# A direct dependency on ScalarE in place of a one-element copy ahead of two late loads in a softmax kernel

## The chip, the cores and the metric

One core of one Trainium2 chip. The metric is the device time of one execution in microseconds, as the median of several executions. All executions told here are counted as fast ones; the one core's granted clock is 1.0 in every record. Execution times of one kernel spread by a few tenths of a microsecond (by 1.6 us in one experiment, and this is said there). The span of a profile runs from the first to the last instruction and is some 1.8 us shorter than the execution time of the same run. Every experiment is compared with the kernel before, run in the same rounds. Where its edit is against the changed kernel, that rests on the two being equal in time.

## The reference, cut to what matters

```python
# x: float32 [16, 1024, 512]
x_scaled = x / 0.5
x_max = np.max(x_scaled, axis=-1, keepdims=True)
exp_x = np.exp(x_scaled - x_max)
return exp_x / np.sum(exp_x, axis=-1, keepdims=True)
```

16384 rows of 512 numbers: 33.55 MB are read and 33.55 MB are written.

## The kernel before

The rows are cut into eight chunks, each 128 partitions by 16 rows (4.19 MB). VectorE takes the row maxima, ScalarE makes the exponentials and their sums, and VectorE and ScalarE together multiply by the reciprocal sums. There are six buffers, so the seventh and eighth chunk reuse the first and the second. SyncE issues the loads and ScalarE issues the stores. The eighth chunk comes in two parts: SyncE loads 15 of its 16 rows as soon as the second buffer is free, and GpSimd loads the last row (one per partition, 0.26 MB) later.

```python
LOADS = [[(0, 4), (4, G)]] + [WHOLE] * 6 + [[(0, G - 1)]]
BLOCKS = [[(0, 4), (4, 8), (8, G)]] + [WHOLE] * 6 + [[(0, 8), (8, G)]]
STORES = [WHOLE] * 8
...
    def load_last_row(signal):
        seen = stats.tile([P, 1], fp32, name="seen", bufs=1)
        copied = nc.gpsimd.tensor_copy(out=seen, in_=signal)
        finished.append(copied.ins.name)
        c = C - 1
        ...
        for p0, p1 in ((P - 2, P), (0, P - 2)):
            part = nc.gpsimd.dma_start(
                out=to[p0:p1], in_=of_[p0:p1], max_dma_last_dim=2 * D
            )
            finished.append(part.ins.name)
...
        for g in rows:                      # in exponentials(i, rows)
            row = chunks[c][:, lo + g, :]
            nc.scalar.activation(
                out=row, in_=row, func=EXP,
                bias=biases[i][:, g : g + 1], scale=2.0,
                accum_out=sums[i][:, g : g + 1],
            )
            if c == BUFS - 1 and g == 10:
                load_last_row(sums[i][:, g : g + 1])
```

The copy's result is never used. Its job is to stand in GpSimd's queue ahead of the two loads and to hold them there until ScalarE has written the sum of row 10 of the sixth chunk. The list `finished` is what a final no-operation on SyncE waits for.

## Time and profile before

| | before |
|---|---|
| execution time, median of 3 runs | 161.86 us (161.72 to 161.98) |
| span of the profile | 160.5 us (of an execution of 162.29 us) |
| VectorE, ScalarE, GpSimd busy | 134.6, 102.2, 1.9 us |
| moved by transfers | 67.13 MB, mean 418 GB/s |

In the profile DVE is VectorE, ACT is ScalarE, POOL is GpSimd and SP is SyncE; a name with q is the engine's instruction queue. A line of the timeline has the start, the length, the engine, the line of the kernel and the operation, and in brackets the idle time before it and what ended that. The main views are shown in the prediction below. One line is added here: the last wait of SyncE's queue, with its total, its number and its longest in us.

```profile
SPq L205 <- DMA out_dram<-xt: 9.5, 1, 9.5
```

It begins just after the seventh chunk's store has landed and ends when the last one has. A store of 4.19 MB in 9.5 us is 441 GB/s, no slower than the stretches of full engines in the prediction's table (417 to 439 GB/s).

### The profile page before, as it was taken

How to read it: one execution, taken by the hardware profiler on the slowest of the kernel's cores; microseconds unless marked ns; L12 is line 12 of the kernel's file. 1: busy time of each engine (PE TensorE's matmuls, PEld its weight loads, DVE VectorE, ACT ScalarE, POOL GpSimd, SP SyncE). 2: the span in 40 equal slices, each digit the busy share in tenths (PEclk: the TensorE clock that was granted, in tenths of full speed). 3: DMA queues.
4: the chain of work that ended last, by engine and by line, in shares of the span. 5: the costliest groups of instructions: out<-in, count | busy, mean ns of one | idle time of the engine just before them, and what ended most of it. 6: DMA issues, size and time to landing. Idle time of an engine off the chain costs nothing.

```text
span 160.5 us, 411 instructions
## 1 busy us (share of the span) xinstructions
DVE 134.6 (84%) x45; ACT 102.2 (64%) x273; POOL 1.9 (1%) x7
## 2 busy tenths in 40 slices
DVE  0607999999999999999999999999999999957000
ACT  3071549069989963998199909991899891790000
POOL 0000000000000000000000000030000000000000
DMA  5999999999989999999999999989999999999994
GB/s 184 470 408 498 400 392 457 457 392 402 506 269 425 490 392 400 506 400 392 490 425 392 474 434 392 490 383 483 422 450 400 400 465 441 392 457 449 400 441 204
DMA packets 2578, 67.13 MB, mean 418 GB/s; under 512 B 328, under 2 KB 328, under 8 KB 400
## 3 DMA queue, kind: packets, MB, share of 16 engines
q1 hardware_dynamic: 1296, 33.29, 49.3%
q10 hardware_dynamic: 1152, 33.55, 48.4%
q0 software_dynamic: 128, 0.26, 0.4%
q14 instruction: 2, 0.02, 0.0%
HBM read 33.55 MB, written 33.55 MB: 418 GB/s over the span
## 4 chain that ended last, share of the span: by engine, by line
DVE 75%; DMA 7%; issue 5%; ACT 3%; SPq 0%
DVE negmax L77 42%; DVE xt L127 31%; DMA xt<-in_x_dram 7%; ACT xt L108 3%; DVE bias L81 1%; DVE recip L125 1%; SPq L68 0%
## 5 line engine op out<-in xcount | busy, mean ns | idle before, releaser
L108 ACT ACTIVATE xt<-xt,bias 128x512 f32<-128x512 f32 x128 | 90.4, 708 | 41.5 <-DVE bias L81 40.6
L77 DVE TENSOR_REDUCE negmax<-xt 128x16 f32<-128x8192 f32 (+2 forms) x11 | 69.9, 6352 | 9.4 <-DMA xt<-in_x_dram 9.4
L127 DVE TENSOR_TENSOR xt<-xt,recip 128x7168 f32<-128x7168 f32 (+2 forms) x11 | 62.0, 5637 | 0.4
L108 ACT ACTIVATION_READ_ACCUMULATOR xt<-xt,bias 128x1 f32 x128 | 23.9, 187 | 0.0
L138 ACT ACTIVATE xt<-xt,recip 128x512 f32<-128x512 f32 x15 | 9.9, 706 | 0.0
L125 DVE RECIPROCAL recip<-sums 128x16 f32<-128x16 f32 (+2 forms) x11 | 2.4, 218 | 1.8 <-ACT xt L108 1.8
L81 DVE TENSOR_SCALAR bias<-negmax 128x16 f32<-128x16 f32 (+2 forms) x11 | 1.9, 173 | 0.4
L52 ACT ACT_TABLE_LOAD x1 | 1.3, 1283 | 0.7 <-PEq L194 0.7
L97 POOL DMA_DIRECT2D xt<-in_x_dram x2 | 1.5, 741 | 0.5 <-issue 0.5
L90 POOL COPY seen<-sums 128x1 f32<-128x1 f32 x1 | 0.2, 184 | 103.6 <-ACT xt L108 103.6
L51 DVE MEMSET warm<- 128x1 f32 x1 | 0.1, 59 | 0.8 <-PEq L194 0.8
L52 ACT ACTIVATE warm<-warm 128x1 f32<-128x1 f32 x1 | 0.2, 202 | 0.0
L194 POOL MEMSET const-float32-0.0<- 128x1 f32 x1 | 0.1, 93 | 0.2 <-issue 0.2
L194 POOL MEMSET const-bfloat16-1.0<- 128x1 bf16 x1 | 0.1, 95 | 0.0
L194 POOL MEMSET const-uint8-127<- 128x1 uint8 x1 | 0.1, 95 | 0.0
L194 POOL MEMSET const-float32-1.0<- 128x1 f32 x1 | 0.1, 93 | 0.0
## 6 DMA issues: line engine op xcount, KB each, us to landing
out_dram<-xt ACTq DMA_DIRECT2D x8, 4096.0 KB, 23.1
xt<-in_x_dram SPq DMA_DIRECT2D x6, 4096.0 KB, 34.8
xt<-in_x_dram SPq DMA_DIRECT2D x1, 3840.0 KB, 27.8
xt<-in_x_dram SPq DMA_DIRECT2D x1, 3072.0 KB, 11.6
xt<-in_x_dram SPq DMA_DIRECT2D x1, 1024.0 KB, 4.8
xt<-in_x_dram POOLq DMA_DIRECT2D x1, 252.0 KB, 15.4
xt<-in_x_dram POOLq DMA_DIRECT2D x1, 4.0 KB, 9.1
```

The source lines that it names most:

```text
L51: nc.vector.memset(warm, 0.0)
L52: nc.scalar.activation(out=warm, in_=warm, func=EXP)
L77: nc.vector.tensor_reduce(negmax[:, 0:b], chunks[c][:, lo:hi, :], axis=AX, op=MAX, negate=True)
L81: nc.vector.tensor_scalar_mul(biases[i][:, 0:b], negmax[:, 0:b], 2.0)
L90: copied = nc.gpsimd.tensor_copy(out=seen, in_=signal)
L97: part = nc.gpsimd.dma_start(out=to[p0:p1], in_=of_[p0:p1], max_dma_last_dim=2 * D)
L108: nc.scalar.activation(out=row, in_=row, func=EXP, bias=biases[i][:, g : g + 1], scale=2.0, accum_out=sums[i][:, g : g + 1],)
L125: nc.vector.reciprocal(recips[i][:, 0:b], sums[i][:, 0:b])
L127: last = nc.vector.tensor_mul(rows, rows, recips[i][:, 0:k].unsqueeze(2).broadcast_to((P, k, D)))
L138: last = nc.scalar.activation(out=row, in_=row, func=COPY, scale=recips[i][:, g : g + 1])
L194: nc = _bacc.Bacc("TRN2", target_bir_lowering=False, num_devices=1)
```

## The change

The copy goes, and with it GpSimd's only arithmetic in the loop. Both loads are given a dependency on the exponential by hand. The intent is a shorter way from ScalarE to the loads and an engine less that reads memory.

```diff
     def load_last_row(signal):
-        seen = stats.tile([P, 1], fp32, name="seen", bufs=1)
-        copied = nc.gpsimd.tensor_copy(out=seen, in_=signal)
-        finished.append(copied.ins.name)
         c = C - 1
 ...
             part = nc.gpsimd.dma_start(
                 out=to[p0:p1], in_=of_[p0:p1], max_dma_last_dim=2 * D
             )
+            tc.add_manual_dep(part.ins, signal, info, reason="in step")
             finished.append(part.ins.name)
 ...
-            nc.scalar.activation(
+            exponential = nc.scalar.activation(
 ...
             if c == BUFS - 1 and g == 10:
-                load_last_row(sums[i][:, g : g + 1])
+                load_last_row(exponential.ins.name)
```

(The definition of `info` moves from the end of the kernel to its start.)

More of the change, by code (lines that the diff above doesn't have):

```diff
@@ L59 @@
     finished = []
+    info = mybir.DependencyInfo(
+        mybir.DependencyClass.Sync, mybir.DependencyReason.DATA
+    )
     def load(c):
@@ L174 @@
     seen = nc.sync.nop()
-    info = mybir.DependencyInfo(
-        mybir.DependencyClass.Sync, mybir.DependencyReason.DATA
-    )
     for name in finished:
```

## The prediction

> **What bounds the kernel now.** I read the page first, then the transfer shares by stretch, then the chain of the end, then what waits on GpSimd. The page says that two things are full at once:
>
> ```profile
> span 160.5 us, 411 instructions
> DVE 134.6 (84%) x45; ACT 102.2 (64%) x273; POOL 1.9 (1%) x7
> DMA  5999999999989999999999999989999999999994
> HBM read 33.55 MB, written 33.55 MB: 418 GB/s over the span
> DVE 75%; DMA 7%; issue 5%; ACT 3%; SPq 0%
> ```
>
> The reader is to see that the transfers are at nine tenths or more in nearly every slice, and that GpSimd (POOL) is busy for 1.9 us of 160.5. The chain of the end gives 75% to VectorE (DVE), but a chain goes back from an instruction to its releaser; it doesn't show a queue of transfers that is never empty. For that I cut the span by hand, at the times where the late loads and the last store begin and land (columns: stretch, length, busy time of DVE, ACT and POOL, clock, DMA share, GB/s):
>
> ```profile
> 88.00:104.09 16.09, 16.02 (x5) 12.08 (x35) 0.00 (x1) 1.00 1.01 434
> 104.82:106.30 1.48, 1.48 (x1) 1.48 (x5) 1.48 (x2) 1.00 0.97 417
> 106.30:120.90 14.60, 14.53 (x5) 10.59 (x29) 0.00 (x0) 1.00 1.02 436
> 120.90:132.83 11.93, 11.86 (x5) 11.44 (x30) 0.00 (x0) 1.00 1.02 439
> ...
> 140.00:147.48 7.48, 5.57 (x3) 4.46 (x12) 0.00 (x0) 1.00 0.98 425
> 147.48:150.10 2.62, 0.00 (x0) 0.00 (x0) 0.00 (x0) 1.00 0.93 400
> 150.10:159.70 9.60, 0.00 (x0) 0.00 (x0) 0.00 (x0) 1.00 0.88 379
> ```
>
> From 88 us on the 16 engines move 417 to 439 GB/s without a gap. The last store (4.19 MB) is issued at 147.48 and lands 12.2 us later, at about 159.7. From 147.48 to 159.70 the table gives 2.62 us x 400 + 9.60 us x 379 = 4.69 MB, some 0.5 MB more than that store: an estimate of what the store before it still had to move when it was issued, a good microsecond at 434 GB/s. So VectorE, which ends at 147.4, and the transfers reach the end together; neither alone would give much back.
>
> The part that is changed, in order of time:
>
> ```profile
> 103.84 0.18 ACT L108 ACTIVATION_READ_ACCUMULATOR xt<-xt,bias 128x1 f32 x1
> 103.86 8.68 DVE L77 TENSOR_REDUCE negmax<-xt 128x16 f32<-128x8192 f32 x1
> 103.93 0.71 ACT L108 ACTIVATE xt<-xt,bias 128x512 f32<-128x512 f32 x1
> 104.09 0.18 POOL L90 COPY seen<-sums 128x1 f32<-128x1 f32 x1 [103.64 <-ACT xt L108]
> ...
> 104.82 1.48 POOL L97 DMA_DIRECT2D xt<-in_x_dram  x2 [0.55 <-issue]
> ```
>
> The exponential of row 10 of the sixth chunk delivers its sum at 103.84 + 0.18 = 104.02. The copy starts 0.07 us later and ends at 104.27; then GpSimd sits idle for 0.55 us for nothing that the profile shows, and makes the descriptors of its two loads until 106.30. The row these loads bring is needed only by the last row maximum, which starts at 132.83:
>
> ```profile
> xt<-in_x_dram POOLq DMA_DIRECT2D x1, 252.0 KB, 15.4
> xt<-in_x_dram POOLq DMA_DIRECT2D x1, 4.0 KB, 9.1
> L77 DVEq EVENT_SEMAPHORE  x1: 21/21/21, 125.3 to 125.3; - x1
> L205 POOLq DRAIN  x3: 40/103/15775, 105.3 to 160.2; - x3
> 132.83 4.41 DVE L77 TENSOR_REDUCE negmax<-xt 128x8 f32<-128x4096 f32 x1
> ```
>
> The larger load, issued at 105.5, lands 15.4 us later, at 120.9; the drain on GpSimd's queue agrees (105.3 + 15.8 = 121.1). VectorE's only separate semaphore wait at that line, at 125.3, lasts 21 ns: what it asks for is there already. So the load is 4.4 us ahead of the check and 132.83 - 120.9 = 11.9 us ahead of use. That is the slack that everything below must be held against.
>
> **What the Trainium skill says.** First, "DMA: Bandwidth & Descriptors", section "Issuing engines are not separate DMA queues": transfers issued from ScalarE, SyncE or GpSimd all run on the same 16 engines and interleave, and issuing from several only saves issue time. The trace agrees: the rate is 417 to 439 GB/s with GpSimd's queue in use and without. Second, the same page's "Specifications" gives a ceiling of 435 GB/s for the fabric; the 434 to 439 here (a few per cent of rounding at the cut edges) are at it. Third, "SBUF — State Buffer", section "Who interferes with whom": a VectorE instruction with two SBUF inputs contends with a GpSimd instruction that reads SBUF, while a reduction doesn't contend. The copy reads SBUF, and VectorE's two-input product ended at 96.32 + 7.62 = 103.94, just before the copy; during the descriptors VectorE runs a reduction. So no clash shows in this trace, and none is there to be removed. Fourth, "Perfetto Trace Analysis", section "DMA Instruction — SWDGE (GPSIMD)": the profile's end of such an instruction is the last descriptor written, not the data's landing. The trace agrees: 0.70 and 0.78 us for the instructions, against 9.1 and 15.4 us to landing.
>
> **The change part by part.** (1) Removed: one copy of 128x1, 0.18 us on GpSimd, which is idle for 103.6 us before. On the path of the end: 0. VectorE and ScalarE don't wait for it; the waits list has no waiter on GpSimd's copy. (2) Moved: the wait for ScalarE goes from the copy to the loads themselves. It is the same event at the same 104.02, since the copy too was released by this exponential. The loads also had to wait for the second chunk's store, which was over by about 88 us (the SyncE queue issued the other fifteen rows into the same buffer at 88.0); that wait stays and costs nothing. (3) The issue of the first load: at least the copy's 0.18 us goes. Of the 0.55 us of idle after it, part is the queue's own semaphore instruction (43 ns) and presumably the decoding of the load, which stays. So the first descriptors start between 104.1 (all goes: 0.73 us earlier) and 104.65 (only the copy goes); I choose 104.5, about 0.3 us earlier. If nothing else moves, the larger load lands at 120.6 rather than 120.9, and its slack grows from 11.9 to 12.2 us. Value at the end: 0. (4) Transfers: the same 0.26 MB in the same 128 packets, out of 67.13 MB. With the engines full before and after, 0.3 us earlier for 0.4% of the bytes only trades places with bytes of the loads and stores beside it. (5) The final wait on SyncE has one item less to wait for, the copy. It waits for the seventh chunk's store until 150.1 anyway, and the program's end waits on the last store until 159.7. Value: 0. (6) The start-up fills of constants on GpSimd (four of 0.09 us) stay, so the start doesn't move. Sum on the path: 0 + 0 + 0 + 0 + 0 = 0 us, out of 161.86.
>
> **The rivals.** (a) The order is lost: if the new dependency held only one load, or none, the loads would go at about 88 us, when the buffer comes free, 16 us earlier. For it: the dependency is now set by hand, not implied by data. Against it: the final wait is set in the same way and does hold in this trace. Its effect: the queue is as full at 88 us (434 GB/s) as at 104, so bytes trade places again; the other fifteen rows land a little later, still before 125.3. Within 0.3 us of now, either sign. (b) The copy was a cushion: without it the descriptors could run into VectorE's product, and stall or slow it. The product ends at 103.94 and the release is at 104.02, so the margin is under 0.1 us, but ScalarE's schedule decides it and is not changed. If they met, the skill's section speaks of reads only, and descriptors are written; at worst 0.7 us on VectorE, of which about one microsecond of queued store hides most. To 162.3 at most. (c) A change of order among transfers opens a gap. Between 116 and 125 us only the fifth chunk's store and these loads are in flight, and the next store comes at 125.43; the bytes are the same, so a gap would be there before too. Worth under 0.2 us. (d) The path of the end does run through GpSimd in a way that the profile hides; then up to 0.73 us would be saved: 161.1. The 11.9 us of slack speak against it.
>
> **Range and chances.** The sum is zero, so the prediction is the time before, 161.86, rounded to 161.8. The three runs spread from 161.72 to 161.98; other executions and the rivals add about as much again on either side: 161.5 to 162.2 should hold it 8 times in 10. A change of 2% is 3.2 us, over four times all that the change can move on GpSimd. No rival reaches it. Faster by over 2%: 0.01; within 2%: 0.98; slower by over 2%: 0.01.
>
> **What would show it.** GpSimd is to have 6 busy instructions instead of 7, about 1.7 us, and no copy; its first load starts between 104.1 and 104.65 and is now said to wait for ScalarE. Its larger load lands at 120.2 to 120.8. VectorE's last reduction starts at 132.8, the last store is issued at 147.5 and the DMA row is unchanged. Wrong would be: loads at 88 us (rival a), a product of 128x7168 longer than 7.63 us next to the descriptors (rival b), a DMA share under 0.95 between 116 and 126 us (rival c), or an end moved by as much as the loads (rival d).

## The result, and the profile after

| | before | after |
|---|---|---|
| median of 6 runs | 161.88 us (161.72 to 161.99) | 162.07 us (161.80 to 162.44) |
| ratio after to before, 95% interval | | 1.0013 (0.9997 to 1.0029) |
| span of the profile | 160.5 us (execution of 162.29 us) | 160.5 us (execution of 162.30 us) |
| GpSimd busy | 1.9 us, 7 instructions | 1.7 us, 6 instructions |

A ratio here and below is the mean time of one kernel's fast runs over that of the other's of the same rounds, so it isn't quite the ratio of the medians quoted. The interval contains 1: no change is shown.

The page of the changed kernel, in the lines that answer to those of before (busy time by engine, the transfers' row of 40 slices, and the two late loads with KB and us from issue to landing):

```profile
DVE 134.6 (84%) x45; ACT 102.2 (64%) x273; POOL 1.7 (1%) x6
DMA  5999999999999999999999999999999999999993
xt<-in_x_dram POOLq DMA_DIRECT2D x1, 252.0 KB, 15.9
xt<-in_x_dram POOLq DMA_DIRECT2D x1, 4.0 KB, 9.1
```

The timeline around the changed place:

```profile
103.88 0.19 ACT L109 ACTIVATION_READ_ACCUMULATOR xt<-xt,bias 128x1 f32 x1
103.90 8.68 DVE L80 TENSOR_REDUCE negmax<-xt 128x16 f32<-128x8192 f32 x1
...
104.36 1.47 POOL L97 DMA_DIRECT2D xt<-in_x_dram  x2 [103.92 <-ACT xt L109]
...
132.86 4.41 DVE L80 TENSOR_REDUCE negmax<-xt 128x8 f32<-128x4096 f32 x1
```

And three lines of what the instruction queues did: GpSimd's separate semaphore instructions of the loads (length in ns as least, median, longest; first and last start), its drain at the end in the same form, and SyncE's last wait:

```profile
L97 POOLq EVENT_SEMAPHORE  x2: 17/30/42, 87.4 to 87.5; - x2
```

```profile
L203 POOLq DRAIN  x3: 40/107/16265, 104.9 to 160.3; - x3
```

```profile
SPq L203 <- DMA out_dram<-xt: 9.5, 1, 9.5
```

The copy is gone and the loads now name ScalarE as what released them. ScalarE's sum is there at 103.88 + 0.19 = 104.07, and descriptors begin at 104.36: 0.29 us, against 0.80 us before (104.02 to 104.82). The wait for the buffer's store has been moved ahead, to 87.4, so the load itself waits for ScalarE alone. But the larger load, issued at 105.1, takes 15.9 us in place of 15.4 and lands at 121.0, not earlier than the 120.9 of before; the drain agrees (104.9 + 16.3 = 121.2). Nothing that lies behind it moved: the last reduction starts at 132.86 (before: 132.83) and SyncE's last wait is 9.5 us in both. So in these traces the half microsecond was won on GpSimd, spent again in the engines' queues, and would have been worth nothing at the end in any case.

### The profile page after: what moved, and what is told of

Read it like the earlier page. It is cut to its first block, busy times and chain, and to the rows that moved or that the text cites. A ratio compares the mean times of both kernels' runs of the same rounds, so it can differ in the third digit from the quotient of the medians.

```text
span 160.5 us, 411 instructions
## 1 busy us (share of the span) xinstructions
DVE 134.6 (84%) x45; ACT 102.2 (64%) x273; POOL 1.7 (1%) x6
## 4 chain that ended last, share of the span: by engine, by line
DVE 75%; DMA 7%; issue 5%; ACT 3%; SPq 0%
DVE negmax L80 42%; DVE xt L128 31%; DMA xt<-in_x_dram 7%; ACT xt L109 3%; DVE bias L84 1%; DVE recip L126 1%; SPq L71 0%
## 6 DMA issues: line engine op xcount, KB each, us to landing
xt<-in_x_dram POOLq DMA_DIRECT2D x1, 252.0 KB, 15.9
```

## The experiments

The theory: the late loads are off the path that sets the end, with some 12 us of slack, and the end is set by transfers that never pause, with VectorE close behind. The rivals: a path through GpSimd that the profile doesn't show, a cost of the time at which these loads enter, and a clash of GpSimd with VectorE.

### The changed kernel again

No edit.

> The changed kernel once more, for a narrower interval. Theory (the late loads have 11.9 us of slack, and the engines that move data are full either way): ratio 1.000, between 0.998 and 1.002, and the larger late load lands at about 121 us whether its issue is at 104.4 or 104.8. Rival (the first six runs, 162.07 against 161.88, show a real cost of the change): ratio 1.0013 again with the interval above 1.0000.

Measured: 161.85 us (161.70 to 161.90, 5 runs) against 161.94 us (161.84 to 162.13, 9 runs), ratio 0.9991 (0.9979 to 1.0004). The first table's +0.1% is not repeated; its sign turns. Both intervals contain 1. The difference of the first table is noise as far as these runs can tell. The larger late load's time from issue to landing is repeated: 15.8 us, with the landing at 120.8.

### No step at all

```diff
-            tc.add_manual_dep(part.ins, signal, info, reason="in step")
```

> The dependency on the exponential is taken away; the late loads wait only until the store of their buffer has landed. Theory: they are issued at about 88 us, 16 us earlier, land at 98 to 108 us, and the time stays within 0.3 us of 161.9, because the same bytes go through full engines. Rival (the step is there because early loads push back the load beside them or the stores): slower by 1 us or more, with the other fifteen rows landing after 125.3 us or VectorE waiting for a transfer.

Measured: 162.22 us (162.08 to 162.32) against the same 161.94, ratio 1.0014 (1.0002 to 1.0027). The timeline, and the page's line of the larger load:

```profile
88.37 1.47 POOL L97 DMA_DIRECT2D xt<-in_x_dram  x2 [87.92 <-DMA out_dram<-xt]
```

```profile
xt<-in_x_dram POOLq DMA_DIRECT2D x1, 252.0 KB, 21.0
```

The loads go 16 us earlier. The larger one, issued at 89.1, needs 21.0 us and lands at 110.1, later than the 98 to 108 expected, and the time is 0.28 us longer by the medians, within the 0.3 us expected; the interval is just clear of 1. The rival's full microsecond isn't there, and VectorE waits for no transfer but the two at the start that every run has (9.5 us in all). This is what the kernel would do if the new dependency had been lost: next to nothing.

### Thirty-two copies in place of one

```diff
-        copied = nc.gpsimd.tensor_copy(out=seen, in_=signal)
+        for _ in range(32):
+            copied = nc.gpsimd.tensor_copy(out=seen, in_=signal)
```

> The kernel before with 32 copies of the sum in place of one. At 0.18 us each, 31 more are 5.6 us, so the loads are issued at about 110.5 us. Theory: the larger load lands at 122 to 129 us, before its use at 132.8, and the time is unchanged, ratio 0.998 to 1.002. Rival (the end runs through GpSimd): plus up to 5.6 us, 167.5 us.

Measured: 161.81 us (161.68 to 161.91), ratio 0.9991 (0.9978 to 1.0005).

```profile
104.11 7.76 POOL L91 COPY seen<-sums 128x1 f32<-128x1 f32 x32 [103.66 <-ACT xt L109]
112.42 1.48 POOL L98 DMA_DIRECT2D xt<-in_x_dram  x2 [0.56 <-issue]
...
132.84 4.41 DVE L77 TENSOR_REDUCE negmax<-xt 128x8 f32<-128x4096 f32 x1
```

```profile
xt<-in_x_dram POOLq DMA_DIRECT2D x1, 252.0 KB, 13.1
```

The thirty-two copies take 7.76 us, some 0.24 us each and not 0.18, and push the loads to 112.42, past the 110.5 expected. The larger one is issued at 113.1, needs 13.1 us and lands at 126.2, still before the last reduction, which starts at 132.84 as ever. GpSimd's part was made 7.6 us longer (112.42 against 104.82) and the end didn't move: the interval contains 1. The rival of a hidden path through GpSimd falls here: taking 0.5 us from GpSimd cannot help where adding 7.6 us doesn't hurt. The idle 0.56 us between the last copy and the loads is there again as it was with one copy.

### No late loads

```diff
-    LOADS = [[(0, 4), (4, G)]] + [WHOLE] * 6 + [[(0, G - 1)]]
+    LOADS = [[(0, 4), (4, G)]] + [WHOLE] * 7
...
-            if c == BUFS - 1 and g == 10:
+            if False:
```

> No late loads on GpSimd at all: the last chunk comes as one load of 16 rows on the SyncE queue. Theory: 161.9 us within 0.4, since the bytes are the same and the whole load lands at 116 to 119 us, before the check at 125.3. Rival (the late row buys time by leaving the queue to others): slower by over 0.5 us.

Measured: 162.27 us (162.16 to 162.35), ratio 1.0018 (1.0006 to 1.0031). As expected within 0.4 us, but clear of 1. So the whole device of a separate last row on GpSimd is worth at most some 0.3 us here, 0.2%. That is also about the spread of one kernel: the profiled execution of the kernel before, which isn't among the nine, took 162.29 us. With the run without a step it suggests that the row is a little dearer when it goes in at 88 us with the others. What makes these 0.3 us is not settled: VectorE's timing doesn't explain it, since in this run the last store was issued at 147.36, 0.12 us earlier than before.

### The step at row 5: with the copy, and direct

The kernel before and the changed kernel, each with this edit:

```diff
-            if c == BUFS - 1 and g == 10:
+            if c == BUFS - 1 and g == 5:
```

> The kernel before with row 5 in place of row 10 as the trigger, its exponential ending near 100.5, in the middle of VectorE's product of two inputs (96.3 to 103.9). If the copy is shut out by the product: it starts or ends only at 104 and the loads are issued at 104.8 as before. If not: copy at 100.6, loads at 101.3. The time is unchanged in either case, 161.9 within 0.4.

> The changed kernel with row 5 as the trigger, so that descriptors are made while VectorE's product of two inputs runs. Theory[...]: loads at 100.8, 0.7 us each, product still 7.62 us, time unchanged within 0.4 us. Rival b of the prediction: descriptors take until 104, or the product is longer than 7.7 us.

Measured: with the copy 161.81 us (161.75 to 162.06), ratio 0.9992 (0.9977 to 1.0007); direct 161.84 us (161.84 to 162.00), ratio 0.9991 (0.9974 to 1.0008). The times tell nothing; the traces do. With the copy:

```profile
96.22 7.62 DVE L127 TENSOR_TENSOR xt<-xt,recip 128x7168 f32<-128x7168 f32 x1
...
100.47 3.42 POOL L90 COPY seen<-sums 128x1 f32<-128x1 f32 x1 [100.02 <-ACT xt L108]
...
103.83 1.48 POOL L97 DMA_DIRECT2D xt<-in_x_dram  x2
```

Direct:

```profile
96.33 7.62 DVE L128 TENSOR_TENSOR xt<-xt,recip 128x7168 f32<-128x7168 f32 x1
...
100.82 1.47 POOL L97 DMA_DIRECT2D xt<-in_x_dram  x2 [100.37 <-ACT xt L109]
```

The reader is to compare the copy's 3.42 us with its 0.18 us in the kernel before. It begins inside VectorE's product of two inputs and ends at 100.47 + 3.42 = 103.89, the product at 96.22 + 7.62 = 103.84: the copy of 128 numbers was held until the product was over, and the loads behind it with it. This is the exclusive use that the Trainium skill states in "SBUF — State Buffer", section "Who interferes with whom", for a GpSimd instruction that reads. The product was not slowed: 7.62 us in both. The descriptors of the loads, in contrast, take the same 1.47 us in the middle of the product as outside of it. So the clash of the prediction's rival b is real, but it belongs to the copy that was removed and not to the loads. In the kernel before, the copy came 0.15 us after the product's end (104.09 against 103.94), so there was nothing to save at row 10. One more thing shows: behind the held copy the loads follow without the 0.55 us of idle time that they have behind a short one (103.89, then 103.83 as recorded), so that idle time isn't a fixed price of following a copy. What it is stays open.

### The step later than the slack

In the changed kernel, for the two runs:

```diff
-            if c == BUFS - 1 and g == 10:
+            if c == BUFS and g == 10:                      # first run
+            if c == C - 1 and lo == 0 and g == 2:          # second run
```

> The dependency is on row 10 of the seventh chunk, whose exponential ends near 120.7, so the late loads are issued 16.5 us later than in the changed kernel, at about 121 to 122. Theory (slack is to 132.8): the loads by then share the engines with stores only and land near 131 to 134, so the end moves by 0 to 1.5 us. If the landing still took 15.9 us: it is at 137.7 and the end moves by about 4 us.

> The dependency is on row 2 of the last chunk, whose exponential ends near 128.2. Theory: issued at about 129, landing at 138 to 144, after the use at 132.8; VectorE waits 5 to 11 us for the transfer and the time grows by 4 to 10 us, 166 to 172 us. If the late loads had no bearing on the end at any time: 0.

Measured: first 162.94 us (162.19 to 163.80, 4 runs) against 161.96, ratio 1.0060 (1.0013 to 1.0108); second 171.07 us (170.68 to 171.40), ratio 1.0560 (1.0535 to 1.0584). The first, in four views (timeline; the reduction's semaphore instruction; transfers by stretch with columns as in the prediction; the page's line of the larger load):

```profile
121.09 1.47 POOL L97 DMA_DIRECT2D xt<-in_x_dram  x2 [120.65 <-ACT xt L109]
...
135.14 4.42 DVE L80 TENSOR_REDUCE negmax<-xt 128x8 f32<-128x4096 f32 x1 [2.09 <-DMA xt<-in_x_dram]
```

```profile
L80 DVEq EVENT_SEMAPHORE  x1: 21/21/21, 135.1 to 135.1; - x1
```

```profile
147.48:150.10 2.62, 2.23 (x1) 0.00 (x0) 0.00 (x0) 1.00 0.32 138
```

```profile
xt<-in_x_dram POOLq DMA_DIRECT2D x1, 252.0 KB, 13.3
```

The larger load is issued at 121.8 and lands 13.3 us later, at 135.1, a microsecond after the 131 to 134 expected. VectorE now waits for it, and the last reduction is 135.14 - 132.86 = 2.28 us late. The end moves by less. This execution took 163.53 us, 1.2 us more than the profiled one of the changed kernel (162.30) and 1.6 us more than the 161.96, so 0.7 to 1.1 us of the delay were taken up by what the transfers still had in hand when VectorE came late. The stretch from 147.48 us shows them run dry, at a share of 0.32 before the last store is issued at 149.80. SyncE's last wait is 11.0 us in this run in place of 9.5: the last store starts from rest and pays for it. The four executions fall into two pairs, 162.19 and 162.36, 163.53 and 163.80, and only one of the slower pair was profiled. So the 0.98 us by the medians lies between the two, and why they differ is not known.

The second run, timeline:

```profile
128.36 1.47 POOL L97 DMA_DIRECT2D xt<-in_x_dram  x2 [127.91 <-ACT xt L109]
...
142.29 4.42 DVE L80 TENSOR_REDUCE negmax<-xt 128x8 f32<-128x4096 f32 x1 [9.44 <-DMA xt<-in_x_dram]
```

Here the load is on the path: VectorE is 9.4 us late and the time grows by 9.1 us by the medians, by 8.7 us in the profiled execution. Together the two runs measure the slack from the other side. A load issued at 113.1 costs nothing, one issued at 121.8 a microsecond by the medians (0.2 to 1.8 us), one issued some 7 us later 8 us more.

### What sets the end: bytes, VectorE, or both

Three kernels with wrong results, from the changed kernel. The first stores only 12 of the 16 rows of the sixth chunk, the second scales only 4 of 7 rows in VectorE's last product, the third does both:

```diff
             if hi == end:
+                cut = 12 if c == 5 else hi
                 part = nc.scalar.dma_start(
-                    out=outr[c][:, lo:hi, :], in_=chunks[c][:, lo:hi, :]
+                    out=outr[c][:, lo:cut, :], in_=chunks[c][:, lo:cut, :]
```

```diff
         nc.vector.reciprocal(recips[i][:, 0:b], sums[i][:, 0:b])
+        if i == n - 1:
+            k = 4
         rows = chunks[c][:, lo : lo + k, :]
```

> The changed kernel, wrong on purpose: the sixth chunk's store leaves out 4 of 16 rows (1.05 MB, 2.4 us at 434 GB/s). Theory (when the last store is issued the engines have about 0.5 MB left, some 1.2 us): the backlog vanishes, the gain is 0.3 to 1.2 us and no more, since VectorE then sets the end. If transfers alone set the end: minus 2.4 us. If VectorE alone: 0.

> The changed kernel, wrong on purpose: VectorE's very last product takes 4 rows in place of 7, so it is 1.6 us shorter (2.29 us against 3.89) and the last store is issued near 145.9. Theory: the engines are still busy with the store before, so the gain is 0 to 0.6 us. If VectorE alone sets the end: minus 1.6 us.

> Both of these together. Theory (two bounds that reach the end together): more than the sum of the two alone, 1.4 to 2.0 us in all. If one of the two alone sets the end: no more than that one gives by itself.

Measured, against 161.96 us (161.77 to 162.42, 11 runs):

| | median | ratio, 95% interval | mean change |
|---|---|---|---|
| fewer bytes | 161.20 us | 0.9949 (0.9936 to 0.9961) | -0.8 us |
| VectorE 1.6 us shorter | 161.89 us | 0.9995 (0.9981 to 1.0008) | -0.1 us, not told from 0 |
| both | 159.47 us | 0.9845 (0.9829 to 0.9861) | -2.5 us |

(The mean change is the ratio less 1, times 161.96.) With fewer bytes, the stretch before the last store and SyncE's last wait:

```profile
140.00:147.48 7.48, 5.64 (x3) 4.53 (x12) 0.00 (x0) 1.00 0.80 346
```

```profile
SPq L204 <- DMA out_dram<-xt: 11.1, 1, 11.1
```

With VectorE shorter, the issue of the last store and the same wait:

```profile
145.96 0.34 ACTq L151 DMA_DIRECT2D out_dram<-xt  x1
```

```profile
SPq L205 <- DMA out_dram<-xt: 9.4, 1, 9.4
```

The engines run dry before 147.48 when bytes are taken away (share 0.80, 346 GB/s), the last wait grows to 11.1 us, and only 0.8 of the 2.4 us is won: from there on VectorE sets the end. When VectorE is made 1.6 us shorter the last store is issued at 145.96, but its bytes wait behind the store before it, the last wait stays at 9.4 us, and nothing is won. With both, 2.5 us are won, far more than 0.8 + 0.1 and about all that the bytes are worth (2.4 us), and the last wait is 9.5 us again. That is what two bounds close together look like: transfers in front, VectorE some 0.8 us behind. The third run's gain is above the 1.4 to 2.0 us expected. One thing is mixed into the first and third: their shortened store no longer waits for ScalarE's last two rows, so it is issued 4.7 us earlier (120.74 against 125.46). In the first one's trace the store before it lands only at 130.4, and the engines are full until then (share 1.02 from 120.74 to 130.40), so little can have come of the earlier issue.

### The last store in two halves

```diff
-    STORES = [WHOLE] * 8
+    STORES = [WHOLE] * 7 + [[(0, 8), (8, G)]]
```

> The changed kernel with the last chunk's store in two halves, the first issued when its rows are scaled, near 142. Correct results. Theory: the engines have work without a gap, and only the backlog and the fixed cost of the last store can be won: 0.2 to 1.5 us faster. If the end is set by the bytes alone: 0.

Measured: 162.08 us (161.82 to 162.33), correct, ratio 1.0001 (0.9987 to 1.0015). The expected gain isn't there. The first half is issued at 143.91, not near 142, and goes in behind a store that keeps the engines full, so an earlier issue has nothing to win: the answer that was foretold for an end set by bytes. No correct version tried here is shown to be faster than the two kernels.

## Why the prediction was right or wrong

The measured median of 162.07 us lies in the predicted 161.5 to 162.2, though two of the six executions, 162.30 and 162.44, lie above it. The time is the same, which was given 0.98. (The sum's 161.86 should have been rounded to 161.9, not to 161.8.)

1. **The removed copy is worth nothing at the end**: shown. Adding 31 copies costs nothing either.
2. **The issue of the first load**: 104.36 in the trace, in the stated 104.1 to 104.65 and 0.14 us before the 104.5 chosen. Of the 0.55 us of idle time after the copy some 0.3 us went too.
3. **The larger load lands at 120.6**: wrong. It lands at 121.0, as late as before. The step took the time from issue to landing as fixed, and it isn't: issued at 101.5, 104.5, 105.1 and 105.5 (direct at row 5, copy at row 5, changed, before) the load lands 19.2, 16.0, 15.9 and 15.4 us later, at 120.7, 120.5, 121.0 and 120.9. Four microseconds of issue time move the landing by at most half a microsecond. In these runs the landing seems to be set by what else is in the engines' queues. The traces give two hints. In all four the store of the fourth chunk, issued near 92.2, lands within about 0.2 us of the load (in the kernel before it is issued at 92.18 and lands 28.8 us later, at 120.9). And the load took 21.0 us where it shared the engines with a load and a store nearly all the way (issued at 89.1), 13.1 to 13.3 us where it had only stores beside it for most or all of the way (issued at 113.1 and later; SyncE's fifteen rows land at about 115.7). No run was made to test how they share.
4. **The slack of 11.9 us**: in kind right, shown by the two late steps. Issuing later shortens the way to landing (13.1 to 13.3 us from 113 us on), so in issue time the slack is larger than that number.
5. **The 21 ns of VectorE's semaphore instruction show that the load is there**: the conclusion held, the ground didn't. In the run of the late step the same instruction lasts 21 ns as well although VectorE waited 2.09 us for the load. Its length says nothing here, which agrees with what the Trainium skill says in "Perfetto Trace Analysis", section "Sequencer-only Instruction (DRAIN, etc)": the time in the wait isn't recorded. What tells is when it starts, 125.3 in both kernels and 135.1 with the late step. The last section shows an instruction of the kernel before that doesn't follow the page.
6. **The half megabyte left when the last store is issued, a good microsecond**: right in kind, the size less sure than it looked. The same sum over the trace of the changed kernel gives half of it, 2.62 us x 450 + 9.60 us x 338 = 4.42 MB, some 0.2 MB over the store or half a microsecond:

```profile
147.48:150.10 2.62, 0.00 (x0) 0.00 (x0) 0.00 (x0) 1.00 1.05 450
150.10:159.70 9.60, 0.00 (x0) 0.00 (x0) 0.00 (x0) 1.00 0.78 338
```

   The experiments give 0.8 us (bytes taken away) and 0.7 to 1.1 us (VectorE made late, in the profiled execution). "Neither alone would give much back" is shown by the table of three. Sharper than the prediction had it, transfers are in front, and VectorE alone gives nothing.
7. **Rival a** (order lost) didn't happen, and forced it costs 0.28 us by the medians, inside the 0.3 us allowed. **Rival b** (clash with the product) exists for the copy, not for the loads. **Rival c**: no gap opened, the share of the transfers between 116 and 126 us is 1.01 before and after. Its ground was misread, though: until 120.9 the fourth chunk's store was in flight as well, not only the fifth's and the late loads. **Rival d**: refuted by the copies.

## What to carry to other kernels

Before shortening a wait, ask when its result is used: here 12 us of slack lay behind 0.5 us of saving, and 7.6 us of added delay cost nothing. A chain of the end that names a compute engine doesn't show transfers that never pause; look whether the last store's bytes follow directly on those before (here a last wait of 9.5 us for 4.19 MB), and take a little from each bound alone and from both together before working on either. A copy that only carries a signal is still a reader of memory: on GpSimd it was held by VectorE's two-input product, 3.42 us in place of 0.18, and the loads behind it with it. The direct dependency escapes that, though no time was gained by it here.

## What the Trainium skill lacked or had wrong

- "DMA: Bandwidth & Descriptors", section "Anatomy of one DMA — SWDGE (gpsimd) path", gives about 2.0 us plus bytes over 436 GB/s, from which 2.6 us is the estimate for 252 KB. Issued into engines that are full, the same load took 13.1 to 21.0 us here, and one of 4 KB 9.1 us in both kernels. The page has a rule for the turns of the queues, but no figure for how long a small load waits for its share.
- "SBUF — State Buffer", section "Who interferes with whom", says that a two-input product contends with GpSimd's reads. Of an earlier probe it says, without a number, that such a product didn't stall a transfer, and the reason it only infers. Here both have numbers: copy 0.18 to 3.42 us, two loads' descriptors 1.47 us inside and outside of the product.
- No page found gives the cost of letting a GpSimd load wait itself against putting an instruction ahead of it: from ScalarE's sum to the first descriptor 0.29 us against 0.80 us.
- "Perfetto Trace Analysis", section "Sequencer-only Instruction (DRAIN, etc)", leaves the wait for a semaphore out of what is recorded. VectorE's 21 ns agree. One of the six semaphore instructions in SyncE's queue at the end of the kernel before doesn't: it starts at 106.9 and lasts 8.85 us, until 115.8, when SyncE's fifteen rows have landed (88.0 + 27.8). The two other runs with a copy each have one too (9.2 and 9.0 us), which also end when those rows have landed. So a long one can contain a wait, though a short one doesn't show that there was none.

```profile
L174 SPq EVENT_SEMAPHORE  x6: 27/28/8854, 106.9 to 150.1; - x6
```
